# Softmax times V on one core: two heads side by side on the partitions, in two score buffers of 64 KB

## The chip, the cores and the metric

The kernel runs on one core of a Trainium2 chip. A core has a matrix engine (TensorE: PE in the profile, PEld for its weight loads), a vector engine (VectorE, DVE), an activation engine (ScalarE, ACT), a general engine (GpSimd, POOL), and a queue (SyncE, SP) that here issues every DMA; 16 DMA engines carry the transfers. SBUF and PSUM are addressed by 128 partitions. The metric is the device time of one execution in microseconds, the median of several runs.

## The reference

```python
batch, n_heads, seq, head_dim = 8, 12, 1024, 64      # scores: (8, 12, 1024, 1024), v: (8, 12, 1024, 64), float32
def reference(scores, v):
    scores_max = np.max(scores, axis=-1, keepdims=True)
    attn = np.exp(scores - scores_max)
    attn = attn / (np.sum(attn, axis=-1, keepdims=True) + 1e-8)
    return np.matmul(attn, v).astype(np.float32)
```

There are 96 heads. Each has 4 MB of scores, 256 KB of v and 256 KB of output.

## The kernel before

The kernel exponentiates the scores without subtracting the maximum, in fp16, and divides by the row sums after the product with v; a column of ones beside v gives the sums. It notes the extremes of the sums and of v, and if a later test (`judge`, then `count`) says that they left the range in which this is safe, a slow general path (`general`) runs instead. With these inputs it does not.

A loop over 24 iterations handles four heads each (`AHEAD = 4`, k = 0 to 3). Each head has a score buffer `s_nat[k]` of 128 partitions by 8 rows of 1024 (32 KB a partition; partition p holds 8 adjacent rows of the head). For each head, with r from 0 to 7 (one "row" is 128 score rows, one on each partition):

- ScalarE exponentiates two rows at a time from `s_nat` into one of 8 buffers `p_nat` (L414); for the last head of an iteration, from its third row on, one row at a time.
- TensorE turns the eight 128x128 blocks of a row into a PSUM bank `psT` (L427, four buffers). The identity used, `order16`, also puts even partitions first and odd ones behind.
- VectorE copies the bank to `pt` in SBUF (L434, four buffers).
- Three rows later (`LAG = 3`), `finish` multiplies: eight products of 128x65 into `psO` (L173), which collects four rows in a bank (`G = 4`).
- After four rows, VectorE takes reciprocals of the sums (L150) and scales (L158): two instructions of 64 partitions x 256 each, into `out_sb`, which holds two heads.

POOL spreads v from the form in which it was loaded (`v_sb`, four heads in 1 MB) to `vones[k]`, an fp16 copy with ones (`spread_v`, L270: four copies a head). `watch_v` (L287) reduces each `vones[k]` to its largest magnitude on VectorE, for the test.

SP's queue issues in an order written out by hand (`queue`): load of head 0 and of head 1 for the next iteration, the store of the heads 0 and 1, load of head 2, v, load of head 3, the store of the heads 2 and 3. A load into `s_nat[k]` waits until ScalarE has read the whole buffer, and each load is one DMA of 4 MB. Only in the last iteration but one are the heads 2 and 3 of the last iteration loaded in parts: 4, 4, then 3, 2, 1, 1 and 1 rows (`last`). In the last iteration, `end` scales the last head by ScalarE (L216) and VectorE (L219) and stores its output in two DMAs (L227).

TensorE's instructions are kept in program order (`in_line`). At the end of an iteration `judge` computes a count on VectorE and TensorE, and ScalarE loads its table again when the next begins (ACT_TABLE_LOAD).

Of the kernel before, what the change touches and what calls it, by code (L numbers as in the profile page):

```python
# [26 lines left out]
def kernel(  # L27
# [14 lines left out]
    R = SQ // P  # L42
    C = SK // P
    M = D + 1
    EB = 2
    G = 4
# [5 lines left out]
    T = 2  # L52

    sc_bh = scores.rearrange("b h (p r) j -> (b h) p r j", p=P)
    v_bh = v.rearrange("b h (i t) d -> (b h i) (t d)", i=Q)  # L60


    W = P // T
    out_bh = out.rearrange("b h (j x) d -> (b h j) (x d)", j=W)

# [6 lines left out]
    order16 = const_pool.tile([P, P], FP16, name="order16")  # L72

    nc.vector.tensor_copy(
        out=order16[:].rearrange("p (t j) -> p t j", t=T),
        in_=ident32[:].rearrange("p (j t) -> p t j", t=T),
    )


    vones_bufs = []  # L80
    for k in range(AHEAD):
        vo = const_pool.tile([P, C, D + 2], FP16, name=f"vones{k}")
        nc.vector.memset(vo[:, :, D : D + 2], 1.0)
        vones_bufs.append(vo)


# [10 lines left out]
    seen = small_pool.tile([P, 1 + AHEAD * R + 1], FP32, name="seen")  # L97
    nc.vector.memset(seen, 1.0)
    done = small_pool.tile([P, R * D], FP32, name="done")
    v_seen = small_pool.tile([P, 1 + AHEAD + 1], FP32, name="v_seen")  # L100
    nc.vector.memset(v_seen, 1.0)
    psT_bufs = buffers(ps_pool, 4, [P, SK], FP16, "psT")


    psO_bufs = buffers(ps_pool, 2 * (R // G), [P, 512], FP32, "psO")
# [32 lines left out]
    def one(bh, n):  # L138
        return bh[bass.ds(n, 1)].rearrange("o p r d -> (o p) r d")

    def sums(k, st, b):

        psO = st["psO"][b][:, 0 : G * M].rearrange("p (g m) -> p g m", m=M)
        at = 1 + k * R + b * G
        recip = seen[:, at : at + G].rearrange("p (g o) -> p g o", o=1)
        return psO, recip

    def invert(k, st, b):
        psO, recip = sums(k, st, b)
        return nc.vector.reciprocal(out=recip, in_=psO[:, :, D : D + 1])  # L150

    def normalise(k, st, b):

        psO, recip = sums(k, st, b)
        h = k % T
        for t in range(T):
            part = slice(t * W, (t + 1) * W)
            nc.vector.tensor_tensor(  # L158
                out=st["out_sb"][h * W : (h + 1) * W, t, b * G : (b + 1) * G, :],
                in0=psO[part, :, 0:D],  # L160
                in1=recip[part].to_broadcast([W, G, D]),
                op=mybir.AluOpType.mult,
            )

    def finish(u):

        n0, k, r, pt, st = u
        b, g = r // G, r % G
        if r == 0:
            st["out_sb"] = out_bufs[k // T]  # L170
        bank = st["psO"][b]
        for c in range(C):
            product = nc.tensor.matmul(  # L173
                out=bank[:, g * M : (g + 1) * M],
                lhsT=pt[:, c * P : (c + 1) * P],
                rhs=st["vones"][:, c, 0:M],
                start=(c == 0),
                stop=(c == C - 1),
            )
            in_line(product)  # L180
        if g == G - 1 and k < AHEAD - 1:
            invert(k, st, b)
            normalise(k, st, b)
        if r == R - 1:
            spread_v(k)
            if k == T - 1:
                store(n0, 0)

    def store(n0, k):

        to = out_bh.rearrange("(m x) y -> m x y", x=P)[bass.ds((n0 + k) // T, 1)]
        to = to.rearrange("o x y -> (o x) y")
        of = out_bufs[k // T][:].rearrange("x t r d -> x (t r d)")
        send(nc.sync.dma_start(out=to, in_=of))
# [9 lines left out]
    def end(st):  # L204


        k, h = AHEAD - 1, (AHEAD - 1) % T
        send(
            nc.sync.dma_start(
                out=out_bh[(BH - T) * W : (BH - T + h) * W],  # L210
                in_=out_bufs[k // T][0 : h * W].rearrange("x t r d -> x (t r d)"),
            )
        )
        psO, recip = sums(k, st, 0)
        for g in range(G):
            nc.scalar.mul(done[:, g * D : (g + 1) * D], psO[:, g, 0:D], recip[:, g, :])  # L216
        invert(k, st, 1)
        psO, recip = sums(k, st, 1)
        nc.vector.tensor_tensor(  # L219
            out=done[:, G * D :].rearrange("p (g d) -> p g d", d=D),  # L220
            in0=psO[:, :, 0:D],
            in1=recip.to_broadcast([P, G, D]),
            op=ALU.mult,
        )
        to = out_bh[(BH - 1) * W : BH * W].rearrange("j (t y) -> t j y", t=T)
        for t in range(T):
            send(nc.sync.dma_start(out=to[t], in_=done[t * W : (t + 1) * W]))  # L227

    stores = []
    writers = {}  # L230
# [14 lines left out]

    def load(k, n, parts=(R,), r=0, **cond):
        for rows in parts:
            queue(
                nc.sync.dma_start(  # L249
                    out=s_bufs[k][:, r : r + rows, :],  # L250
                    in_=one(sc_bh, n)[:, r : r + rows, :],
                    **cond,
# [14 lines left out]
    def spread_v(k):  # L267

        for s in range(S):
            spread = nc.gpsimd.tensor_copy(  # L270
                out=vones_bufs[k][s * Q : (s + 1) * Q, :, 0:D].rearrange(
                    "i (h l) d -> i h l d", l=L
                ),
                in_=v_sb[k * Q : (k + 1) * Q, :, s],
            )
            for watch in watches:
                apart(spread, watch, "products in between")

    def spread_of(tile, n):

        nc.vector.tensor_reduce(out=tile[:, 0:1], in_=tile[:, 0 : n + 1], axis=X, op=ALU.min)  # L281
        nc.vector.tensor_reduce(  # L282
            out=tile[:, n + 1 : n + 2], in_=tile[:, 1 : n + 2], axis=X, op=ALU.max
        )

    def watch_v(k, behind):
        watch = nc.vector.tensor_reduce(  # L287
            out=v_seen[:, 1 + k : 2 + k],
            in_=vones_bufs[k][:, :, 0:D],
            axis=mybir.AxisListType.XY,  # L290
# [5 lines left out]

    def within(out, tile, n, low, high, also=None):
        part = small("part")
        if also is None:
            nc.vector.tensor_scalar(  # L300
                out=part, in0=tile[:, n + 1 : n + 2], scalar1=high, scalar2=None, op0=ALU.is_le
            )
        else:
            nc.vector.scalar_tensor_tensor(  # L304
                out=part, in0=tile[:, n + 1 : n + 2], scalar=high, in1=also,
                op0=ALU.is_le, op1=ALU.mult,
            )
        nc.vector.scalar_tensor_tensor(  # L308
            out=out, in0=tile[:, 0:1], scalar=low, in1=part, op0=ALU.is_ge, op1=ALU.mult
        )  # L310
# [190 lines left out]
```

## Time and profile before

| | |
|---|---|
| median of 3 runs | 1067.54 us (1067.52 to 1068.3) |
| profiled execution | 1067.78 us; its span 1066.0 us |
| granted TensorE clock, mean | 0.825 |
| HBM read, written | 436.21 MB, 25.17 MB; 433 GB/s over the span |
| DMA queue q1 | 99.1% of 16 engines' span |
| busiest engine, VectorE | 786.2 us (74%) |
| ScalarE | 741.1 us (70%) |

The span runs from the first to the last instruction of the profiled execution; the execution's time also holds what lies around it. In the page's second part each digit is the busy share of one of 40 slices of the span, in tenths. In its fourth part the chain is followed backwards from the last instruction. A group's row gives the line, the engine, the operation, what it writes and reads, the count, then the busy time, the mean duration in ns, and the idle time of the engine just before with what ended it. In a time line the first two numbers are the start and the length in us, and brackets give the idle time before it and what ended it.

### The profile page before, as it was taken

How to read it: one execution, taken by the hardware profiler on the slowest of the kernel's cores; microseconds unless marked ns; L12 is line 12 of the kernel's file. 1: busy time of each engine (PE TensorE's matmuls, PEld its weight loads, DVE VectorE, ACT ScalarE, POOL GpSimd, SP SyncE). 2: the span in 40 equal slices, each digit the busy share in tenths (PEclk: the TensorE clock that was granted, in tenths of full speed). 3: DMA queues.
4: the chain of work that ended last, by engine and by line, in shares of the span. 5: the costliest groups of instructions: out<-in, count | busy, mean ns of one | idle time of the engine just before them, and what ended most of it. 6: DMA issues, size and time to landing. Idle time of an engine off the chain costs nothing.

```text
span 1066.0 us, 33658 instructions
## 1 busy us (share of the span) xinstructions
PE 727.3 (68%) x12312; PEld 692.9 (65%) x12312; DVE 786.2 (74%) x1660; ACT 741.1 (70%) x484; POOL 244.8 (23%) x406
## 2 busy tenths in 40 slices
PE   2766866677766667676676766767766667666775
PEld 2766756666766667666675766667765667666674
DVE  1876867868678677776777777868677677786786
ACT  3756776666867668586676776666767668586685
POOL 3113212131121311212113211131121311212113
PEclk9888888878788888887888888878788787887888
DMA  9999999999999999999999999999999999999995
GB/s 393 431 423 434 424 438 430 432 432 428 432 433 433 429 436 433 433 433 432 434 427 439 433 433 433 431 435 432 433 432 433 422 440 433 432 432 427 434 427 206
DMA packets 25014, 453.08 MB, mean 425 GB/s; under 512 B 2800, under 2 KB 2800, under 8 KB 9392
## 3 DMA queue, kind: packets, MB, share of 16 engines
q1 hardware_dynamic: 25008, 453.00, 99.1%
q8 instruction: 4, 0.07, 0.0%
q14 instruction: 2, 0.02, 0.0%
HBM read 436.21 MB, written 25.17 MB: 433 GB/s over the span
## 4 chain that ended last, share of the span: by engine, by line
DMA 61%; PE 11%; PEld 8%; ACT 5%; DVE 5%; issue 4%; POOL 2%; SPq 1%; POOLq 1%; ACTq 0%; DVEq 0%
DMA s_nat<-in_scores_dram 61%; PE psT L427 6%; ACT p_nat L414 5%; PE psO L173 5%; PEld L427 5%; DVE pt L434 5%; PEld L173 4%; POOL vones L270 2%; SPq L261 1%; SPq L249 0%; POOLq L270 0%; POOLq L385 0%; POOLq L461 0%; POOLq L389 0%; DVE out_sb L158 0%
## 5 line engine op out<-in xcount | busy, mean ns | idle before, releaser
L414 ACT ACTIVATE p_nat<-s_nat 128x2048 f16<-128x2048 f32 (+1 forms) x456 | 709.4, 1630 | 219.0 <-DMA s_nat<-in_scores_dram 173.2
L427 PE MATMUL psT<-order,p_nat 128*128 128x128 f16 x6144 | 570.3, 251 | 227.5 <-ACT p_nat L414 216.3
L434 DVE COPY pt<-psT 128x1024 f16<-128x1024 f16 x768 | 513.9, 687 | 189.1 <-PE L173 77.3
L427 PEld LDWEIGHTS <-p_nat 128*128 128x128 f16 x6144 | 461.3, 125 | 244.8 <-ACT p_nat L414 232.6
L270 POOL CAST vones<-v_sb 32x512 f16<-32x512 f32 x400 | 244.1, 610 | 814.1 <-PE L427 385.0
L173 PE MATMUL psO<-vones,pt 128*128 128x65 f16 x6144 | 358.5, 205 | 34.6 <-DVE pt L434 33.0
L173 PEld LDWEIGHTS <-pt 128*128 128x128 f16 x6144 | 301.2, 106 | 48.7 <-DVE pt L434 42.6
L158 DVE TENSOR_TENSOR out_sb<-psO,seen 64x256 f32<-64x256 f32 x380 | 160.2, 422 | 63.6 <-DMA out_dram<-out_sb 52.4
L414 ACT ACT_TABLE_LOAD x24 | 30.8, 1283 | 94.1 <-PE psO L173 52.8
L287 DVE TENSOR_REDUCE v_seen<-vones 128x1 f32<-128x512 f16 x96 | 65.1, 679 | 0.8
L324 PE MATMUL psO<-vones,right 128*1 128x1 f16 x24 | 3.9, 164 | 69.2 <-DVE right L308 69.2
L324 PEld LDWEIGHTS <-right 128*1 128x1 f16 x24 | 1.9, 79 | 72.2 <-DVE right L308 72.2
L150 DVE RECIPROCAL seen<-psO 128x4 f32<-128x4 f32 x192 | 33.7, 176 | 8.6 <-PE psO L173 8.6
L308 DVE SCALAR_TENSOR_TENSOR right<-seen,part 128x1 f16<-128x1 f32 x24 | 10.5, 437 | 0.8
L308 DVE SCALAR_TENSOR_TENSOR fits<-v_seen,part 128x1 f32<-128x1 f32 x24 | 10.0, 415 | 0.0
L328 DVE CAST count<-psO 1x1 int32<-1x1 f32 x24 | 3.5, 146 | 6.2 <-PE psO L324 6.2
L304 DVE SCALAR_TENSOR_TENSOR part<-seen,fits 128x1 f32<-128x1 f32 x24 | 4.6, 192 | 0.8
L281 DVE TENSOR_REDUCE seen<-seen 128x1 f32<-128x33 f32 x24 | 4.5, 187 | 0.8
L281 DVE TENSOR_REDUCE v_seen<-v_seen 128x1 f32<-128x5 f32 x24 | 3.8, 159 | 0.7
L282 DVE TENSOR_REDUCE seen<-seen 128x1 f32<-128x33 f32 x24 | 4.2, 177 | 0.0
L282 DVE TENSOR_REDUCE v_seen<-v_seen 128x1 f32<-128x5 f32 x24 | 3.6, 149 | 0.0
L300 DVE TENSOR_SCALAR part<-v_seen 128x1 f32<-128x1 f32 x24 | 3.5, 144 | 0.0
(12 smaller groups left out, 2.8 us busy)
## 6 DMA issues: line engine op xcount, KB each, us to landing
s_nat<-in_scores_dram SPq DMA_DIRECT2D x96, 4096.0 KB, 32.3
v_sb<-in_v_dram SPq DMA_DIRECT2D x24, 1024.0 KB, 18.5
out_dram<-out_sb SPq DMA_DIRECT2D x47, 512.0 KB, 26.2
s_nat<-in_scores_dram SPq DMA_DIRECT2D x2, 2048.0 KB, 31.3
s_nat<-in_scores_dram SPq DMA_DIRECT2D x1, 1536.0 KB, 32.2
s_nat<-in_scores_dram SPq DMA_DIRECT2D x3, 512.0 KB, 20.7
s_nat<-in_scores_dram SPq DMA_DIRECT2D x1, 1024.0 KB, 25.1
out_dram<-out_sb SPq DMA_DIRECT2D x1, 256.0 KB, 3.0
```

The lines of the kernel that those rows point to most:

```text
L150: return nc.vector.reciprocal(out=recip, in_=psO[:, :, D : D + 1])
L158: nc.vector.tensor_tensor(out=st["out_sb"][h * W : (h + 1) * W, t, b * G : (b + 1) * G, :], in0=psO[part, :, 0:D], in1=recip[part].to_broa ...
L173: product = nc.tensor.matmul(out=bank[:, g * M : (g + 1) * M], lhsT=pt[:, c * P : (c + 1) * P], rhs=st["vones"][:, c, 0:M], start=(c == 0) ...
L261: nc.sync.dma_start(out=v_sb[:].rearrange("x h s l d -> x (h s l d)"), in_=rows[bass.ds(n // AHEAD, 1)].rearrange("o x y -> (o x) y"),)
L270: spread = nc.gpsimd.tensor_copy(out=vones_bufs[k][s * Q : (s + 1) * Q, :, 0:D].rearrange("i (h l) d -> i h l d", l=L), in_=v_sb[k * Q : ( ...
L281: nc.vector.tensor_reduce(out=tile[:, 0:1], in_=tile[:, 0 : n + 1], axis=X, op=ALU.min)
L282: nc.vector.tensor_reduce(out=tile[:, n + 1 : n + 2], in_=tile[:, 1 : n + 2], axis=X, op=ALU.max)
L287: watch = nc.vector.tensor_reduce(out=v_seen[:, 1 + k : 2 + k], in_=vones_bufs[k][:, :, 0:D], axis=mybir.AxisListType.XY, op=ALU.max, appl ...
L308: nc.vector.scalar_tensor_tensor(out=out, in0=tile[:, 0:1], scalar=low, in1=part, op0=ALU.is_ge, op1=ALU.mult)
L414: exp = nc.scalar.activation(out=p_nat[:, g : g + rows, :].rearrange("p r (x v) -> p x r v", v=Q * L), in_=s_bufs[k][:, r + g : r + g + ro ...
L427: turned = nc.tensor.transpose(out=psT[:, c * P : (c + 1) * P], in_=p_row[:, c // L, c % L, :], identity=order16[:],)
L434: copy = nc.vector.tensor_copy(out=pt[:], in_=psT[:])
```

## The change

Two heads now lie beside each other: partitions 0 to 63 hold one head and 64 to 127 the next, with 16 adjacent score rows on each partition. So there are two buffers of 128 x 16 x 1024 (64 KB a partition, 8 MB) instead of four of 32 KB, and an iteration of four heads has two passes, k = 0 and 1 (`K = 2`), of R = 16 rows.

- A load is one DMA of 8 MB. The first, before the loop, comes in halves; the last, for k = 1 of the last iteration, in 4, 4, 3, 2, 1, 1, 1 rows. SP's order is now: load of k = 0, its store, load of k = 1, its store, v.
- `vones` is one tile with the values of both heads of a pass side by side, each with its ones. A product is 128x130: every score row is multiplied by both heads' values, and only the half that belongs to its head is read afterwards.
- Three rows of 130 columns fill a bank of `psO` (`G = 3`), so a pass has six groups, the last of one row. Each group has a reciprocal and two scalings, 64 partitions x 192 (or x 64).
- `psT` and `pt` become two buffers of two rows each (two banks of PSUM), and VectorE copies two rows in one instruction, but for the last eight rows of k = 1, which are exponentiated and copied one at a time.
- `order16` gives way to a plain identity. `watch_v` becomes one reduction over all of `vones` in each iteration with two small tests behind it. The last pass is scaled by the ordinary `normalise`, and stored in two DMAs: 12 rows, then 4.

```diff
-    R = SQ // P
-    G = 4
+    G = 3
+    K = AHEAD // T
+    W = P // T
+    R = SQ // W
+    N = D + 2
+    M = T * N - 2
+    GROUPS = -(-R // G)
...
-    s_bufs = buffers(sb_pool, AHEAD, [P, R, SK], FP32, "s_nat")
+    s_bufs = buffers(sb_pool, K, [P, R, SK], FP32, "s_nat")
...
-    pt_bufs = buffers(sb_pool, 4, [P, SK], FP16, "pt")
-    out_bufs = buffers(sb_pool, 2, [P, T, R, D], FP32, "out_sb")
+    pt_bufs = buffers(sb_pool, 2, [P, EB, SK], FP16, "pt")
+    out_bufs = buffers(sb_pool, K, [P, R, D], FP32, "out_sb")
...
-    psT_bufs = buffers(ps_pool, 4, [P, SK], FP16, "psT")
+    psT_bufs = buffers(ps_pool, 2, [P, EB, SK], FP16, "psT")
...
-                rhs=st["vones"][:, c, 0:M],
+                rhs=vones[:, k, c].rearrange("p t n -> p (t n)")[:, 0:M],
...
-        if g == G - 1 and k < AHEAD - 1:
-            invert(k, st, b)
-            normalise(k, st, b)
-        if r == R - 1:
+        if i == G - 1 or r == R - 1:
+            normalise(k, st, g)
+        if r == R - 1 and k < K - 1:
             spread_v(k)
-            if k == T - 1:
-                store(n0, 0)
+            store(n0, k)
...
             with tc.If(n0 < BH - 2 * AHEAD) as cmp2:
                 queued[:] = before
-                load(AHEAD - 2, (n0 + (2 * AHEAD - 2)) % BH)
-                load_v((n0 + 2 * AHEAD) % BH)
-                load(AHEAD - 1, (n0 + (2 * AHEAD - 1)) % BH)
-                store(n0, AHEAD - T)
+                load(k, (n0 + (AHEAD + T * k)) % BH)
+                store(n0, k)
+                load_v((n0 + 2 * AHEAD) % BH)
             with cmp2.Else():
                 queued[:] = before
-                load(AHEAD - 2, BH - 2, (4, 4))
-                load(AHEAD - 1, BH - 1, (3,))
-                store(n0, AHEAD - T)
-                load(AHEAD - 1, BH - 1, (2, 1, 1, 1), 3)
+                load(k, BH - T, (4, 4, 3))
+                store(n0, k)
+                load(k, BH - T, (2, 1, 1, 1), 11)
...
+                late = k == K - 1 and r >= R // 2
                 if r % EB == 0:
-                    p_nat = take(p_bufs)
-                    rows = 1 if k == AHEAD - 1 and r > 0 else EB
+                    p_nat, psT2, pt2 = take(p_bufs), take(psT_bufs), take(pt_bufs)
+                    rows = 1 if late else EB
...
-                copy = nc.vector.tensor_copy(out=pt[:], in_=psT[:])
-                rewrite(pt, copy)
...
+                if late:
+                    copy = nc.vector.tensor_copy(out=pt, in_=psT)
+                    rewrite(pt2, copy)
+                    other_bank(psT2, r % EB, copy)
+                elif r % EB == EB - 1:
+                    copy = nc.vector.tensor_copy(out=pt2[:], in_=psT2[:])
+                    rewrite(pt2, copy)
+                if k == 0 and r == R // 2 - 1:
+                    watch_v(copy)
+                if r == R - 1 and k < K - 1:
+                    load(k, (n0 + (AHEAD + T * k)) % BH, cond=n0 < BH - AHEAD)
```

More of the change, by code (lines that the diff above doesn't have):

```diff
@@ L158, in normalise @@
             nc.vector.tensor_tensor(
[L159 to L162, printed above, removed]
+                out=out_bufs[k][part, g * G : g * G + rows, :],
+                in0=psO[part, :, t * N : t * N + D],
+                in1=recip[part].to_broadcast([W, rows, D]),
+                op=ALU.mult,
             )
@@ L295, in watch_v @@
         watches.append(watch)
[L297 to L301, printed above, removed]
-            )
[L303 to L310, printed above, removed]
+        for bound, op in ((V_MIN, ALU.is_ge), (V_MAX, ALU.is_le)):
+            nc.vector.scalar_tensor_tensor(
+                out=fits, in0=most, scalar=bound, in1=fits, op0=op, op1=ALU.mult
+            )
     def small(name, dtype=FP32):
@@ L449, in heads @@
             finish(pending.pop(0))
-        last(n0, st)
-        spread_of(seen, AHEAD * R)
+        last(n0)
         judge(st["psO"][-1])
-    assert BH % AHEAD == 0 and BH >= 2 * AHEAD and SK == Q * S * C
+    assert BH % AHEAD == 0 and BH >= 2 * AHEAD and SK == Q * S * C and K == 2
     load_v(0)
-    for k in range(AHEAD):
-        load(k, k)
-    for k in range(AHEAD):
+    for k in range(K):
+        load(k, T * k, (R // 2, R // 2) if k == 0 else (R,))
+    for k in range(K):
         spread_v(k)
@@ L466 @@
         heads(n0)
-    good = nc.values_load(count[:], min_val=0, max_val=P)
+    good = nc.values_load(
+        count[:], min_val=0, max_val=P,
+        skip_runtime_bounds_check_because="a count of partitions, which is compared and no address",
+    )
     with tc.If(good < P, preferred_fallthrough_block=False):
```

207 lines of the change are left out of this document (87 added, 120 removed).

## The prediction

> **What bounds the kernel now.** I read the page first, for the busy shares and the DMA row.
>
> ```profile
> PE 727.3 (68%) x12312; PEld 692.9 (65%) x12312; DVE 786.2 (74%) x1660; ACT 741.1 (70%) x484; POOL 244.8 (23%) x406
> DMA  9999999999999999999999999999999999999995
> DMA packets 25014, 453.08 MB, mean 425 GB/s; under 512 B 2800, under 2 KB 2800, under 8 KB 9392
> DMA 61%; PE 11%; PEld 8%; ACT 5%; DVE 5%; issue 4%; POOL 2%; SPq 1%; POOLq 1%; ACTq 0%; DVEq 0%
> s_nat<-in_scores_dram SPq DMA_DIRECT2D x96, 4096.0 KB, 32.3
> ```
>
> No engine is full; the DMA is, in 39 of 40 slices. A 4 MB load takes 32.3 us from issue to landing, although it moves in about 9.7 us: over 20 us of other transfers are queued ahead of it. Then the chain in order of time, near its end, which gives the period.
>
> ```profile
> 938.44 27.30 DMA s_nat<-in_scores_dram
> 965.85 1.92 ACT p_nat L414
> ...
> 982.31 27.11 DMA s_nat<-in_scores_dram
> 1009.53 1.92 ACT p_nat L414
> ```
>
> The fourth load of an iteration lands at 965.74 and, one iteration on, at 1009.42: 43.68 us. An iteration moves four loads of 4.194 MB, two stores of 0.524 MB and one v load of 1.049 MB, 18.87 MB, so 432 GB/s. At that rate a load is 9.71 us, a store 1.21, v 2.43. What a transfer costs is thus its bytes, and the end of the program is the end of this stream plus what the engines still have to do when the last data come. The time line of ScalarE shows that part.
>
> ```profile
> 1009.53 7.60 ACT L414 ACTIVATE p_nat<-s_nat 128x2048 f16<-128x2048 f32 x7 [4.85 <-DMA s_nat<-in_scores_dram]
> 1020.40 1.28 ACT L414 ACT_TABLE_LOAD   x1 [3.27 <-PE psO L173]
> 1021.69 7.32 ACT L414 ACTIVATE p_nat<-s_nat 128x2048 f16<-128x2048 f32 x4
> 1030.09 17.50 ACT L414 ACTIVATE p_nat<-s_nat 128x2048 f16<-128x2048 f32 x10 [1.08 <-PE psT L427]
> 1048.45 4.85 ACT L414 ACTIVATE p_nat<-s_nat 128x1024 f16<-128x1024 f32 x5 [0.87 <-PE L173]
> ```
>
> The last iteration starts its exponentials at 1021.69, when its first head has landed (1009.42 + a store + a load = 1020.3) and the table is loaded. From there ScalarE hardly rests, and no wait names a DMA: the last iteration is a compute run, and its start decides the end. Its last normalisation and store:
>
> ```profile
> 1057.10 0.42 DVE L219 TENSOR_TENSOR done<-psO,seen 128x256 f32<-128x256 f32 x1
> 1057.60 1.12 SPq L227 DMA_DIRECT2D out_dram<-done  x2
> ```
>
> So first exponential to last product scaled is 1057.52 - 1021.69 = 35.83 us, and 8.5 us more to the span's end at 1066.0. That execution took 1067.78 us, 1.78 more than its span; the median is 0.24 lower.
>
> **Loads in pieces of 8 MB.** Per iteration the same bytes move, in two score loads instead of four. In mid-run the question is whether the queue stays fed. Pair A lands at t; its eight exponentials of two rows are 8 x 1.9 = 15.2 us (7.32 us for four in a row makes it 14.6), so A's buffer is free and its next load issued at about t + 15.7. The queue meanwhile brings B (19.42, behind a store), then a store and v (3.64), and needs A's next load at t + 24.3. The lead is 8.5 us, against more than 20 before. For B, whose second half is eight one-row exponentials (0.965 us each: 139.0/144), 4 x 1.83 + 8 x 0.965 = 15.0, and the lead is about 8. The store of k = 0 stands ahead of B's load on SP, but waits only for products that finish some 6 us after B landed; the v load waits for POOL's 8 copies of 0.61 us behind the last product, and the queue gets to it 20 us later. I cost all this at nothing; what hides it is the 8 us of queued transfers, and each us beyond them would cost up to two us an iteration.
>
> At the end the grain shows. In the stream v(23) now comes behind B of iteration 22, so that B lands at 1009.42 - 2.43 = 1006.99. Behind it come a store, v and the whole 8 MB of A for the last iteration: 1006.99 + 1.21 + 2.43 + 19.42 = **1030.05**. Before, ScalarE had worked since 1021.69 on the first head alone. Now no row of the last 32 can begin before 1030.05: **+8.4 us** on the path. The last B comes in parts, and lands by about 1052 as now, ahead of its use.
>
> **VectorE per iteration.** Rows from the groups by form:
>
> ```profile
> L434 DVE COPY pt<-psT 128x1024 f16<-128x1024 f16 x768 | 513.9, 687 | 189.1 <-PE L173 77.3 <-PE L427 63.3 <-PE psO L173 38.5
> L158 DVE TENSOR_TENSOR out_sb<-psO,seen 64x256 f32<-64x256 f32 x380 | 160.2, 422 | 63.6 <-DMA out_dram<-out_sb 52.4 <-SPq L389 0.7
> L287 DVE TENSOR_REDUCE v_seen<-vones 128x1 f32<-128x512 f16 x96 | 65.1, 679 | 0.8
> L150 DVE RECIPROCAL seen<-psO 128x4 f32<-128x4 f32 x192 | 33.7, 176 | 8.6 <-PE psO L173 8.6
> ```
>
> Reciprocal (4 elements, 176 ns) and scaling (256, 422 ns) give about 1 ns an element and 0.16-0.17 us fixed. A copy of 2048: 1.22 us if the fixed part is paid once, 1.37 if it is two copies; I take 1.22, since the fixed part shows in every row. Copies: 32 x 0.687 = 22.0 becomes 12 x 1.22 + 8 x 0.687 = 20.1 (21.9 at 1.37). Scaling: 16 x 0.422 = 6.8 becomes 20 of 192 at 0.355 and 4 of 64 at 0.222, 8.0. Reciprocals: 8 become 12, +0.7. The watch: 4 x 0.679 = 2.7 becomes one of 2048 elements, 512 at 0.679 scaled, 2.28. The two small tests on fits replace six small ones, -0.1 to -0.4. Sum -1.9 + 1.2 + 0.7 - 0.4 - 0.2 = -0.6, and up to +1.2 with the dear copies; before, copies standing one behind another also overlapped (513.9/768 = 0.669), which fewer, longer ones do less, up to +0.8. I take +0.5, and -0.6 to +2 as bounds. It lies beside the DMA in 23 iterations and on the path in the last.
>
> **TensorE.** 6144 products go from 65 to 130 columns. A transposition of 128 columns is the nearest row: warm, eight take 0.45 us in the chain, against 0.25 for eight products. A row of both goes from 0.70 to 0.90 us, 32 rows to 29 us an iteration; and about double (0.85 for eight transpositions in the chain at 1012.97) for some 4 us behind each wait for data. Under 43.7 us it is hidden. On the path it only adds in the filling of the pipe: a copy now waits for two rows of transpositions, cold 0.85 us more before the first copy; two pairs of buffers instead of four singles let a copy start only when two rows' products are done, which I put at 1 us over the iteration (0 to 2).
>
> **ScalarE** runs 20 exponentials an iteration instead of 19, +0.1 us. The table load stays and lies before the landing.
>
> **Sum.** Last iteration, first exponential to last scaling: 35.83 + 0.5 + 0.85 + 1.0 + 0.1 = 38.3, from 1030.08: 1068.4, where it was 1057.5: +10.8. One last 128 KB store (2.3 us to landing) replaces two issued in turn: -0.6. The four products of ScalarE in end() go, off the path. The start keeps its 4 MB first landing and its wait for POOL's 16 copies: 0. Together +10.2: span 1076.2, execution 1078.0, median about **1077.8**. The other edits (the identity in plain order, the memsets before the loop, the general path, which does not run) touch nothing that the chain names: 0.
>
> Packets double from 32 to 64 KB if they are not split. By the trace's packet records a 4 KB packet lasts 159 ns and a 32 KB one 1213, which leaves 8.4 ns fixed; 8 fewer per engine for each pair, 48 pairs, 3.2 us at most. Loads land 9.68 us apart, which is 1210 ns a packet, so part of it already overlaps. I take 0 and keep -3.2.
>
> The page "SBUF — State Buffer" of the Trainium skill (section on the DMA setup-cost knee) puts about 2 us on every transfer and tells to coalesce: 48 transfers fewer would be 96 us off. The trace does not agree: queued loads of 4 MB land 9.68 us apart, 433 GB/s, with no room for 2 us; it stays as a part of rival 3.
>
> **The rivals.** (1) *VectorE's chain becomes the bound.* Compute alone needs about 38.3 us and 1.3 of table load an iteration, 40 to 41 with the waits between. The first exponential of all is at 18.06; with a compute period P the last iteration starts at 18.06 + 23 P, so it decides from P = (1030.05 - 18.06)/23 = 44.0 on, and each 0.1 us of P is 2.3 us. P of 44.2 to 45.2 gives 1082 to 1105. For: 3 to 4 us of margin, and a cold TensorE at both landings. Against: the work adds only 0.5. 10%.
>
> (2) *The queue runs dry.* If ScalarE is held by 10 us (p_nat released late), 1 to 2 us at 24 reloads: 1102 to 1126. Against: 16 rows of p_nat. 4%.
>
> (3) *The stream itself shortens*, in the s_nat loads, by fewer boundaries between transfers. It must exceed 12.4 us, 0.26 per pair, to end faster than before by our bound; the packet fit gives 3.2. At 0.3 a pair, 14.4: 1063.4. 5%.
>
> (4) *The late grain costs nothing*, since the run was held by something else in the last iteration: then +1 or +2, 1068 to 1069. Against: ScalarE's unbroken row above. 3%.
>
> (5) *The rate falls with the wider address step*: 64 KB between neighbouring partitions. The slowest rate in the trace is that of 4 KB packets, 25.8 GB/s an engine against 27.0 at 32 KB: 4.6% of 931 us of score loads would be 43 us more, 1121. That longer packets only got faster speaks against it. 3%. The Trainium skill's "DMA: Bandwidth & Descriptors" (its table row on HBM row pitch) has 207 against 214 GB/s at a pitch of 512 KiB; no run here shows such a loss.
>
> **How the numbers follow.** Forecast 75%, its own range 1070 to 1086 from the bounds (-3.2 packets, -1.1 VectorE, -1 buffers; upwards the dear copies, buffers, cold rows, 6 to 8). The likeliest is 1077.8. Downwards the range takes in (4) from 1068; upwards the lower half of (1), to 1092; outside lie about 2 in 10. About 0.2%, 2.1 us, is what a measurement can tell from no change: faster 0.05 from (3), same 0.04 from (4) and the edge of the forecast, slower 0.91.
>
> **What would show it.** Right: the DMA row full to the last two slices, iteration period 43.7 us, two landings of 19.4 us each; the last iteration's first exponential at 1030, by a DMA wait; last scaling at 1067 to 1070; copies of 128x2048 at 1.22 us. Wrong: a DMA row with gaps, or periods over 44 (1 or 2); a first exponential of the last iteration well before 1028 (3); a last compute run shorter than 36 us or longer than 42.

## The result: 1074.31 us, and the profile after

The changed kernel takes 1074.31 us (median of 6 runs, 1073.7 to 1074.57); the kernel before, beside it, 1068.38 us (6 runs, 1067.52 to 1069.47). The ratio is 1.0054, 95% interval 1.0044 to 1.0065: slower by 5.9 us, where +10.2 was predicted. The profiled execution took 1074.52 us, its span 1072.8 us (before 1066.0). The spans lie 6.8 us apart, the medians 5.9, since the profiled execution of the kernel before (1067.78) was one of its shorter ones.

The page, its busy shares, the DMA row, the packets, the chain by engine and the loads:

```profile
PE 793.8 (74%) x12312; PEld 757.8 (71%) x12312; DVE 768.7 (72%) x1539; ACT 737.2 (69%) x504; POOL 239.2 (22%) x399
DMA  9999999999999999999999999999999999999991
DMA packets 18436, 453.06 MB, mean 422 GB/s; under 512 B 2048, under 2 KB 2176, under 8 KB 8704
DMA 60%; ACT 27%; issue 7%; PE 2%; DVE 1%; PEld 1%; ACTq 1%; SPq 0%; DVEq 0%
s_nat<-in_scores_dram SPq DMA_DIRECT2D x47, 28.4
```

The DMA is full in the same 39 slices, with the same bytes in 6578 fewer packets. What changed is the chain: ScalarE's share went from 5% to 27%. TensorE is busier by 66.5 us and VectorE less busy by 17.5, and neither bounds the kernel over the whole span. The chain in order of time shows the period and what follows each landing:

```profile
956.97 27.47 DMA s_nat<-in_scores_dram
984.81 1.01 issue
986.30 1.34 issue
987.64 12.72 ACT p_nat L368 x7
1000.58 27.52 DMA s_nat<-in_scores_dram
1028.47 1.01 issue
1029.96 1.34 issue
1031.29 1.91 ACT p_nat L368
```

The first pair of an iteration lands at 984.44 and, one iteration on, at 1028.10 (start and length added). Over many iterations the period is 43.59 us on the mean, against 43.68 before. ScalarE's time line shows what now stands behind each of these landings:

```profile
984.53 1.28 ACT L368 ACT_TABLE_LOAD   x1 [8.10 <-DMA s_nat<-in_scores_dram]
985.83 14.53 ACT L368 ACTIVATE p_nat<-s_nat 128x2048 f16<-128x2048 f32 x8
1005.11 14.91 ACT L368 ACTIVATE p_nat<-s_nat 128x2048 f16<-128x2048 f32 x12 [4.76 <-PE psT L381]
1028.18 1.28 ACT L368 ACT_TABLE_LOAD   x1 [8.17 <-DMA s_nat<-in_scores_dram]
1029.48 29.32 ACT L368 ACTIVATE p_nat<-s_nat 128x2048 f16<-128x2048 f32 x20
```

ScalarE sat idle for 8.17 us ahead of the last iteration and began its exponentials at 1029.48; before, it began at 1021.69. The table load waits for the landing too, so its 1.28 us stand on the path. From there the 20 exponentials run on. VectorE's time line gives the other end of that run:

```profile
1026.39 0.15 DVE L292 CAST count<-psO 1x1 int32<-1x1 f32 x1 [0.26 <-PE psO L288]
1033.38 1.23 DVE L393 COPY pt<-psT 128x2048 f16<-128x2048 f16 x1 [6.84 <-PE L381]
1041.33 2.29 DVE L250 TENSOR_REDUCE most<-vones 128x1 f32<-128x2048 f16 x1
1067.53 0.47 DVE L140 TENSOR_TENSOR out_sb<-psO,seen 64x64 f32<-64x64 f32 x2
```

The count (the last work of iteration 22) is done at 1026.5, so VectorE was 6.8 us idle, too; the first copy starts at 1033.38 and the last scaling ends at 1068.0. The last iteration's first copy before the change:

```profile
1025.45 0.69 DVE L434 COPY pt<-psT 128x1024 f16<-128x1024 f16 x1 [1.30 <-PE L427]
```

The groups by form give the new sizes:

```profile
L393 DVE COPY pt<-psT 128x2048 f16<-128x2048 f16 x288 | 352.4, 1224 | 266.7 <-PE L381 170.0
L140 DVE TENSOR_TENSOR out_sb<-psO,seen 64x192 f32<-64x192 f32 x480 | 170.4, 355 | 14.9
L250 DVE TENSOR_REDUCE most<-vones 128x1 f32<-128x2048 f16 x24 | 54.9, 2286 | 0.8
L152 PE MATMUL psO<-vones,pt 128*128 128x130 f16 x6144 | 486.2, 223 | 63.0 <-DVE fits L260 40.4
```

So the 6.8 us of the span split in three (us):

| stretch | before | after | measured | predicted |
|---|---|---|---|---|
| start to the first exponential of the last iteration | 1021.69 | 1029.48 | +7.8 | +8.4 |
| from there to the end of the last scaling | 35.83 | 38.53 | +2.7 | +2.45 |
| from there to the end of the span | 8.5 | 4.8 | -3.7 | -0.6 |

The first two are near what was foretold; the third is not. It has two parts. The last store landed 3.0 us behind the last scaling before the change (at 1060.49) and 1.9 behind it after (at 1069.91), which is -1.1. The other -2.6 lie between VectorE's branch over the general path and the end of the span: 3.8 us before (from 1062.15), 1.2 after (from 1071.59). VectorE's records show its drain (its next instruction) behind that branch: before at 1065.19, 3.04 us later; after at 1071.81, 0.22 later. That pause is 2.8 us shorter, but not all of it reaches the end, since SyncE's drain now comes behind VectorE's, at 1072.07. The DMA view of the end of each kernel (from 1060 us on; queue and kind: packets, MB, share of the engines) shows what went with it. First before, then after:

```profile
q14 instruction: 2, 0.02, 0.4%
q8 instruction: 1, 0.02, 0.4%
q1 hardware_dynamic: 15, 0.00, 0.1%
```

```profile
q1 hardware_dynamic: 288, 0.52, 8.4%
q8 instruction: 1, 0.02, 0.4%
```

Two packets of 8 KB of instructions on queue q14 (by the records one at 1063.17, in VectorE's pause, and one at 1065.77, 0.6 us behind it) are not there in the changed kernel.

### The profile page after: what moved, and what is told of

The parts are those of the page before. It is cut to its first block, busy times and chain, and to the rows that moved or that the text cites. A ratio compares the mean times of both kernels' runs of the same rounds, so it can differ in the third digit from the quotient of the medians.

```text
span 1072.8 us, 32527 instructions
## 1 busy us (share of the span) xinstructions
PE 793.8 (74%) x12312; PEld 757.8 (71%) x12312; DVE 768.7 (72%) x1539; ACT 737.2 (69%) x504; POOL 239.2 (22%) x399
## 2 busy tenths in 40 slices
DMA packets 18436, 453.06 MB, mean 422 GB/s; under 512 B 2048, under 2 KB 2176, under 8 KB 8704
## 4 chain that ended last, share of the span: by engine, by line
DMA 60%; ACT 27%; issue 7%; PE 2%; DVE 1%; PEld 1%; ACTq 1%; SPq 0%; DVEq 0%
DMA s_nat<-in_scores_dram 60%; ACT p_nat L368 27%; PE psT L381 1%; PE psO L152 1%; ACTq L368 1%; DVE pt L393 1%; PEld L381 0%; PEld L152 0%; DVE most L250 0%; ACT L368 0%; SPq L219 0%; DVE pt L389 0%; DVE out_sb L140 0%; DVE seen L132 0%; DVE seen L276 0%
## 5 line engine op out<-in xcount | busy, mean ns | idle before, releaser
L381 PE MATMUL psT<-ident,p_nat 128*128 128x128 f16 x6144 | 506.0, 233 | 171.0 <-ACT p_nat L368 171.0
L381 PEld LDWEIGHTS <-p_nat 128*128 128x128 f16 x6144 | 425.6, 119 | 181.0 <-ACT p_nat L368 181.0
L393 DVE COPY pt<-psT 128x2048 f16<-128x2048 f16 x288 | 352.4, 1224 | 266.7 <-PE L381 170.0
L152 PE MATMUL psO<-vones,pt 128*128 128x130 f16 x6144 | 486.2, 223 | 63.0 <-DVE fits L260 40.4
L152 PEld LDWEIGHTS <-pt 128*128 128x128 f16 x6144 | 387.3, 99 | 84.8 <-DVE pt L393 55.8
L140 DVE TENSOR_TENSOR out_sb<-psO,seen 64x192 f32<-64x192 f32 (+1 forms) x576 | 191.8, 333 | 18.0
L389 DVE COPY pt<-psT 128x1024 f16<-128x1024 f16 x192 | 123.5, 685 | 2.3
L250 DVE TENSOR_REDUCE most<-vones 128x1 f32<-128x2048 f16 x24 | 54.9, 2286 | 0.8
L132 DVE RECIPROCAL seen<-psO 128x3 f32<-128x3 f32 (+1 forms) x288 | 49.3, 171 | 2.8 <-PE L381 0.8
L260 DVE SCALAR_TENSOR_TENSOR fits<-most,fits 128x1 f32<-128x1 f32 x48 | 7.4, 155 | 0.0
```

The costliest lines, as they stand in the source:

```text
L140: nc.vector.tensor_tensor(out=out_bufs[k][part, g * G : g * G + rows, :], in0=psO[part, :, t * N : t * N + D], in1=recip[part].to_broadcas ...
L152: product = nc.tensor.matmul(out=st["psO"][g][:, i * M : (i + 1) * M], lhsT=pt[:, c * P : (c + 1) * P], rhs=vones[:, k, c].rearrange("p t ...
L250: watch = nc.vector.tensor_reduce(out=most, in_=vones[:, :, :, :, 0:D].rearrange("p k c t d -> p k (c t) d"), axis=mybir.AxisListType.XYZ, ...
L260: nc.vector.scalar_tensor_tensor(out=fits, in0=most, scalar=bound, in1=fits, op0=op, op1=ALU.mult)
L381: turned = nc.tensor.transpose(out=psT[:, c * P : (c + 1) * P], in_=p_row[:, c // L, c % L, :], identity=ident16[:],)
L389: copy = nc.vector.tensor_copy(out=pt, in_=psT)
```

## The experiments

Each kernel was timed in five rounds beside the kernel before, so ratios are to that; differences to the changed kernel use its 1074.31 us. The median of the kernel before lay between 1068.38 and 1068.99 us in the four groups of runs, so such a difference is uncertain by about 0.6 us.

The theory was that the grain of the last loads (how much has to land before work can start) costs about 8 us, that the longer compute run of the last iteration costs 2 to 3, and that the end gains back 3 by something in the way out of the program. Rivals were that the wide products or a slower stream cost part of it.

**1. The first pair's load in halves.** Each load of k = 0 becomes two DMAs of 4 MB.

```diff
-                    load(k, (n0 + (AHEAD + T * k)) % BH, cond=n0 < BH - AHEAD)
+                    load(k, (n0 + (AHEAD + T * k)) % BH, (R // 2, R // 2), cond=n0 < BH - AHEAD)
```

> The changed kernel, but the load of k = 0 comes in two halves of 8 rows in every iteration, as the very first one does. Theory (the grain of the load sets when the last iteration starts): the first half of the last iteration lands some 9.7 us ahead of the second, near 1019; then not the landing but the end of the iteration before (its products at about 1025.5, then the table load) holds the first exponential, which moves from 1029.5 to about 1027; the end comes 2 to 3.5 us earlier, 1071 to 1072. Packets of half of the loads are 32 KB again, which gives back up to 1 us. Rival (the end is set by the end of the DMA stream or by VectorE's total, whenever the run starts): 1074 to 1075.

Measured: 1072.19 us, ratio 1.0034 [1.0022, 1.0046], 2.1 us less than the changed kernel. ScalarE, and then VectorE:

```profile
1006.02 14.91 ACT L368 ACTIVATE p_nat<-s_nat 128x2048 f16<-128x2048 f32 x12 [12.88 <-DMA s_nat<-in_scores_dram]
1020.94 1.28 ACT L368 ACT_TABLE_LOAD   x1
1022.24 24.59 ACT L368 ACTIVATE p_nat<-s_nat 128x2048 f16<-128x2048 f32 x15
```

```profile
1029.05 0.15 DVE L292 CAST count<-psO 1x1 int32<-1x1 f32 x1 [0.26 <-PE psO L288]
1031.36 1.23 DVE L393 COPY pt<-psT 128x2048 f16<-128x2048 f16 x1 [2.16 <-PE L381]
```

The time came as expected, by another way. The exponentials start 7.2 us earlier, at 1022.24, and no longer wait for data. But the second pair of iteration 22 still comes in one piece, and ScalarE starts on it 0.9 us later (1006.02 instead of 1005.11). That iteration now ends later, at 1029.2 on VectorE instead of 1026.5 (the other 1.8 us were not taken apart), and the first copy of the last one gains only 2.0 us. The wait moved from ScalarE to the engines behind it.

**2. The old general path in the changed kernel.** The change also rewrote the general path, which does not run: a fill moved from VectorE to GpSimd, copies and a scaling from VectorE to ScalarE, and its loop got the register-based synchronisation. Here all of that is put back, to find VectorE's shorter pause.

```diff
-        nc.gpsimd.memset(s_bufs[0][:, 3, 0 : C * (D + 1)], 1.0)
+        nc.vector.memset(s_bufs[0][:, 3, 0 : C * (D + 1)], 1.0)
...
-                nc.scalar.copy(out=pt[:, h * half : (h + 1) * half], in_=psO_bufs[h][:, 0:half])
+                nc.vector.tensor_copy(out=pt[:, h * half : (h + 1) * half], in_=psO_bufs[h][:, 0:half])
...
```

> The changed kernel with the general path, which does not run, written as before (its work on VectorE instead of ScalarE and GpSimd, its loop without the register-based synchronisation). Theory (VectorE's jump over the longer general path is what cost 3 us between its branch at 1062.15 and its drain at 1065.19 in the kernel before): 2.5 to 3 us slower, 1077. Rival (the shorter end comes from the left-out bounds check, or from the last stores): 1074.3, no change.

Measured: 1074.61 us, 1.0054 [1.004, 1.0067]. Nothing changed, no pause came back.

**3. The old bounds check of the count.**

```diff
-    good = nc.values_load(
-        count[:], min_val=0, max_val=P,
-        skip_runtime_bounds_check_because="a count of partitions, which is compared and no address",
-    )
+    good = nc.values_load(count[:], min_val=0, max_val=P)
```

> The changed kernel with the bounds check on the loaded count as before. Theory (the jump over the general path): no change, 1074.3, at most +0.5 for the check itself. Rival (the check made the end long): 2.5 to 3 us slower, 1077.

Measured: 1074.75 us, 1.0059 [1.0045, 1.0072]. No pause came back either. The theory that one of these two edits makes VectorE's pause fell.

**4. Products of 65 columns.** This kernel leaves out the products with the other head's values, and so does not compute the reference's output.

```diff
-                rhs=vones[:, k, c].rearrange("p t n -> p (t n)")[:, 0:M],
+                rhs=vones[:, k, c, c % 2, 0 : D + 1],
```

> The changed kernel with products of 65 columns instead of 130: it leaves out the products with the other head's values (the values it takes alternate between the heads, so its output is not the reference's). Theory (VectorE, not TensorE, sets the pace of the last iteration, and in the others the DMA): 0 to 1 us faster, 1073.3 to 1074.3. Rival (the wider products lie on the path of the last iteration, 32 rows of 0.2 us): 4 to 6 us faster, 1068 to 1070.

Measured: 1074.26 us, 1.0052 [1.0039, 1.0066]. The page's busy shares:

```profile
PE 680.1 (63%) x12312; PEld 627.3 (58%) x12312; DVE 768.1 (72%) x1539; ACT 737.3 (69%) x504; POOL 239.2 (22%) x399
```

TensorE is 114 us less busy and the time is the same. Taking both heads' values in each product costs nothing here. The chain of the changed kernel names TensorE from 1051.25 to 1065.72 of the last iteration; by this run that is not where its length comes from, and VectorE's time line has no gap of more than 0.2 us there.

**5. The kernel before with the new general path and without the bounds check.**

```diff
-        nc.vector.memset(s_bufs[0][:, 3, 0 : C * M], 1.0)
+        nc.gpsimd.memset(s_bufs[0][:, 3, 0 : C * M], 1.0)
...
-                nc.vector.tensor_copy(out=pt[:, h * half : (h + 1) * half], in_=psO_bufs[h][:, 0:half])
+                nc.scalar.copy(out=pt[:, h * half : (h + 1) * half], in_=psO_bufs[h][:, 0:half])
...
-    good = nc.values_load(count[:], min_val=0, max_val=P)
+    good = nc.values_load(
+        count[:], min_val=0, max_val=P,
+        skip_runtime_bounds_check_because="a count of partitions, which is compared and no address",
+    )
```

> The kernel before with the general path and the count's load written as in the changed kernel (no bounds check; nothing else changed). Theory (VectorE's 3.0 us between its branch at 1062.15 and its drain at 1065.19 come from these lines, both together): about 2.8 us faster, 1066. Rival (the pause belongs to the layout of the whole program before, for instance the branches of end() and last()): 0 to 0.5 us faster, 1068.4.

Measured: 1068.03 us, 0.9998 [0.9989, 1.0007]. VectorE still pauses, from 1062.35 to 1065.51, with the two packets on q14 (at 1063.64 in the pause and at 1066.09 behind it). Together with 2 and 3: neither edit makes the pause or takes it away.

**6. The grain alone, in the kernel before.** The loads of heads 0 and 1 are issued together, head 1's first, so that the last iteration's first head lands behind both.

```diff
-        if k < AHEAD - 2:
-            load(k, (n0 + (AHEAD + k)) % BH, cond=n0 < BH - AHEAD)
+        if k == 1:
+            for j in (1, 0):
+                load(j, (n0 + (AHEAD + j)) % BH, cond=n0 < BH - AHEAD)
```

> The kernel before with the loads of heads 0 and 1 in the other order in the queue, so that head 0, which every iteration begins with, lands only when both have landed, as with one load of 8 MB. Nothing else changes: products of 65 columns, single copies, packets of 32 KB. Theory (the grain of the first load sets when the last iteration starts): its first exponential moves from 1021.7 to the second landing, 1030.0, or 1031.3 if the table load waits for it too; the run of 35.8 us stays: 8 to 9.7 us slower, 1077 to 1078. Rival (the last iteration's length makes up for a late start, since ScalarE then has both heads at once): 0 to 4 us slower.

Measured: 1077.25 us against 1068.65 in the same job, 1.0083 [1.007, 1.0097]: +8.6 us from the order of two DMAs in each iteration, with the engines' work and every size and packet as before, and the same period (43.68). ScalarE, and VectorE's last scaling:

```profile
1030.62 1.28 ACT L415 ACT_TABLE_LOAD   x1 [12.93 <-DMA s_nat<-in_scores_dram]
1031.91 29.25 ACT L415 ACTIVATE p_nat<-s_nat 128x2048 f16<-128x2048 f32 x19
```

```profile
1066.62 0.42 DVE L219 TENSOR_TENSOR done<-psO,seen 128x256 f32<-128x256 f32 x1
```

It is the picture of the changed kernel: idle until all 8 MB are there, table load behind the landing, then one unbroken run (35.1 us to the end of the last scaling, at 1067.04). The first exponential is 10.2 us later than in the kernel before and the run 0.7 us shorter. This shows that the late first row of the last iteration costs 8 us by itself.

**7. The watch ahead of the first copy.** The reduction over all values (2.29 us) and its two tests move to before the iteration's first copy, where VectorE is idle, from behind the fourth.

```diff
+                    if k == 0 and r == EB - 1:
+                        watch = watch_v()
                     copy = nc.vector.tensor_copy(out=pt2[:], in_=psT2[:])
+                    if k == 0 and r == EB - 1:
+                        after(copy, watch)
                     rewrite(pt2, copy)
-                if k == 0 and r == R // 2 - 1:
-                    watch_v(copy)
```

> The changed kernel with the watch over vones (2.29 us) and its two small tests placed before the first copy of an iteration, where VectorE sits idle, and not behind the fourth copy. Theory (VectorE's work sets the length of the last run): the last scaling comes 2 to 2.5 us earlier, 1072. Rival (ScalarE's exponentials or the products set it): 1073.8 to 1074.3.

Measured: 1072.31 us, 1.0039 [1.0025, 1.0052], 2.0 us less than the changed kernel. VectorE:

```profile
1026.61 0.15 DVE L292 CAST count<-psO 1x1 int32<-1x1 f32 x1 [0.26 <-PE psO L288]
1030.27 2.29 DVE L250 TENSOR_REDUCE most<-vones 128x1 f32<-128x2048 f16 x1 [3.52 <-POOL vones L239]
1033.58 1.22 DVE L395 COPY pt<-psT 128x2048 f16<-128x2048 f16 x1 [0.63 <-PE L381]
```

The watch ends before the first copy could start, and the last scaling ends at 1065.29 instead of 1068.01. From the first exponential (1029.68) that is 35.6 us, no more than before the change. In the last iteration VectorE's work, one instruction behind another, sets the length; with experiment 4, TensorE's does not.

**8. Both old edits at the end together** (2 and 3 in one kernel).

```diff
-                nc.scalar.copy(out=pt[:, h * half : (h + 1) * half], in_=psO_bufs[h][:, 0:half])
+                nc.vector.tensor_copy(out=pt[:, h * half : (h + 1) * half], in_=psO_bufs[h][:, 0:half])
...
-        skip_runtime_bounds_check_because="a count of partitions, which is compared and no address",
```

> The changed kernel with both the general path and the bounds check as before. Theory (both together cause VectorE's pause): 2.5 to 3.5 us slower than 1074.3, 1077 to 1078. Rival (layout of the whole program): at most 0.7 slower, 1075.

Measured: 1075.28 us, 1.0062 [1.0049, 1.0076]; no pause, 1.0 us from the changed kernel, with intervals that overlap. From VectorE's branch to the end of the span it takes 1.7 us where the changed kernel takes 1.2: SyncE, with its check, ends last.

**9. All loads in halves.** As 1, and the loads of k = 1 too, the first one before the loop included.

```diff
-                load(k, (n0 + (AHEAD + T * k)) % BH)
+                load(k, (n0 + (AHEAD + T * k)) % BH, (R // 2, R // 2))
```

> The changed kernel with all loads of 8 MB, of k = 0 and of k = 1, in two halves of 8 rows. Theory (the grain costs twice: the last iteration but one ends late since its k = 1 lands whole, and the last begins late since its k = 0 lands whole): the last iteration's transpositions begin near 1020 instead of 1031, VectorE then needs its 35 to 37 us, last scaling at 1058 to 1061 instead of 1068; with the short end 1065 to 1068, after 2 us more of DMA stream by 32 KB packets. That would be faster than the kernel before. Rival (only the first landing matters, or VectorE's backlog is always there): as with one half, 1071 to 1072.

Measured: 1068.84 us, 1.0003 [0.9994, 1.0012]: 5.5 us less than the changed kernel, level with before, not ahead of it, so the expectation was missed. ScalarE, then VectorE:

```profile
997.50 3.72 ACT L368 ACTIVATE p_nat<-s_nat 128x2048 f16<-128x2048 f32 x2 [3.61 <-PE psT L381]
1007.16 11.31 ACT L368 ACTIVATE p_nat<-s_nat 128x2048 f16<-128x2048 f32 x10 [5.93 <-DMA s_nat<-in_scores_dram]
1020.54 1.28 ACT L368 ACT_TABLE_LOAD   x1 [2.08 <-PE L381]
1021.84 7.32 ACT L368 ACTIVATE p_nat<-s_nat 128x2048 f16<-128x2048 f32 x4
```

```profile
1026.09 0.14 DVE L292 CAST count<-psO 1x1 int32<-1x1 f32 x1 [0.26 <-PE psO L288]
1028.45 1.23 DVE L393 COPY pt<-psT 128x2048 f16<-128x2048 f16 x1 [2.21 <-PE L381]
1062.78 0.47 DVE L140 TENSOR_TENSOR out_sb<-psO,seen 64x64 f32<-64x64 f32 x2
```

The exponentials start at 1021.84, as before the change (1021.69), and the first copy is 4.9 us earlier than in the changed kernel. Two things keep it from more. The packets are 32 KB again and the period is 43.67. And ScalarE stands 5.93 us at the fifth row of iteration 22's second pair (1001.2 to 1007.2), although the first half had landed: in the branch for the last loads the parts are 4, 4 and 3 rows, so one wait that serves all cases must name the second half for row 4.

**10. Forty dead VectorE instructions in the general path of the changed kernel.**

```diff
             nc.vector.reciprocal(out=den, in_=den)
+            for _ in range(40):
+                nc.vector.tensor_scalar(
+                    out=den, in0=den, scalar1=1.0, scalar2=None, op0=ALU.mult
+                )
```

> The changed kernel with 40 more VectorE instructions in the general path, which does not run. Theory (the 3 us pause of the kernel before is a load of instructions: two packets of 8 KB of the kind instruction at 1063.17 and 1065.77, which the changed kernel lacks since VectorE's program is shorter, 128 against 158 instructions): VectorE's jump over the longer path needs such a load, 2.5 to 3.5 us slower, 1077 to 1078, with such packets near the end. Rival (length and distance do not matter): 1074.3 to 1074.7, no packets.

Measured: 1076.41 us, 1.0072 [1.0058, 1.0086], 2.1 us more than the changed kernel (the intervals of the two ratios overlap a little, but the fastest run here, 1076.0, lies above the slowest there, 1074.57). VectorE's records have the pause again, branch at 1071.48 and drain at 1074.33, 2.85 us; its last scaling ends at 1067.89, as without the edit, and the span at 1075.0 instead of 1072.8. The DMA view of its end:

```profile
q8 instruction: 1, 0.02, 0.5%
q14 instruction: 2, 0.02, 0.3%
```

The two packets on q14 are back (one near 1072.5, in the pause, and one near 1074.9, behind it). Only VectorE's program grew, so what went away was a load of its instructions at the jump over the general path; that the packets are VectorE's is read from this and from their times. Built from the kernels of these runs and with every kind of instruction counted (128 and 158 in the expectation are another, smaller count), VectorE's program has 181 instructions in the changed kernel, and 184 and 185 in kernels 2 and 8, all without the pause; it has 220 in the kernel before, 216 in kernel 5 and 261 here, all with it.

**11. Halves, with the last loads cut to match.** As 9, and the last pair's parts are 8 and 3 rows instead of 4, 4 and 3, so that row 4 can wait for the first half.

```diff
-                load(k, BH - T, (4, 4, 3))
+                load(k, BH - T, (R // 2, 3))
```

> As with both loads in halves, but the last load of k = 1 begins with 8 and 3 rows instead of 4, 4 and 3, so that the wait of its fifth row no longer names the second half in every iteration (with both halves ScalarE stood 5.93 us at its fifth row for a DMA). Theory (grain): the last iteration but one ends at 1020 to 1022 instead of 1026, the last scaling near 1058 to 1060 instead of 1063.3; 1064.5 to 1066, faster than the kernel before by 0.25% to 0.4%. Rival (VectorE's backlog, not the landing, ends the last iteration but one): no better than 1068.8.

Measured: 1069.56 us, 1.0006 [0.9997, 1.0015]; the expectation was missed. ScalarE:

```profile
1022.10 1.28 ACT L368 ACT_TABLE_LOAD   x1 [4.83 <-DMA s_nat<-in_scores_dram]
1031.79 7.32 ACT L368 ACTIVATE p_nat<-s_nat 128x2048 f16<-128x2048 f32 x4 [1.07 <-PE psO L152]
1042.86 14.92 ACT L368 ACTIVATE p_nat<-s_nat 128x2048 f16<-128x2048 f32 x12 [3.75 <-PE psT L381]
```

The mended wait did what it was to do: iteration 22 ended at 1022.5 on VectorE, 3.7 us earlier than in kernel 9. But the data came later: the first half of the last k = 0 pair landed at 1022.0, since the period had gone from 43.67 to 43.84 from about the twelfth iteration on, and in the last iteration ScalarE stood 3.75 us until the part of 8 rows had landed (1042.76; the row names TensorE, but the wait of the same length in kernel 12 is put down to the DMA). The last scaling ended at 1063.11, near that of kernel 9 (1063.25).

The landing records say where the period comes from. Each transfer leaves sixteen of them, and it has landed with the last. Up to about the eleventh iteration all sixteen come every 43.67 us. From the twelfth on fifteen still do, and the last falls behind by 0.16 us an iteration: of the first half of the last k = 0 pair, fifteen parts were there by 1020.24 and the sixteenth at 1022.01 (in kernel 9, 1020.32 and 1020.46). So it is not the whole stream that slows but one sixteenth of it, for which every landing waits.

**12. As 11, with the watch behind the second copy.**

```diff
-                if k == 0 and r == R // 2 - 1:
+                if k == 0 and r == 2 * EB - 1:
                     watch_v(copy)
```

> The run before this one in the list, with the watch moved behind the second copy of an iteration, where VectorE waits 1 to 2 us for TensorE. Theory (VectorE sets the length of the last run): 1 to 2 us faster than that run, 1063 to 1065, the fastest of all. Rival: no change to it.

Measured: 1071.96 us (1070.63 to 1073.39; the profile is of the slowest), 1.0028 [1.0018, 1.0038]; missed again, and by the same two steps, larger: a period of 43.94 from the twelfth iteration on, the first half at 1023.3, the part of 8 rows at 1044.07. Again fifteen records of a landing keep 43.67 (fifteen parts of that first half were there by 1020.21), and the last falls behind, here by 0.25 us an iteration. Why one part lags in 11 and 12 is open. Up to iteration 22 they issue the very transfers of kernel 9, so it is not the cut of the transfers: only the engines' waits, with them the moments at which loads are issued, and in 12 the place of the watch differ until then. No version here beat the kernel before; 5, 9 and 11 are level with it.

## Why the prediction was right, and where it was not

- **The grain, +8.4 predicted.** Right in mechanism and nearly in size (+7.8): experiment 6 has it alone, +8.6 us, and 9, with its loads in halves, takes 5.5 us back. Two errors inside the term nearly cancel. "I take 0 and keep -3.2" for the longer packets: the trace's packet records show that 64 KB packets do occur, 5888 of them at 2418 ns (the median) against 2 x 1213 for two of 32 KB, and the period fell by 0.09 us, 2.0 us over 23 iterations; the bound held it, the value did not. And "The table load stays and lies before the landing" is wrong: it waits for the same data and stands behind the landing, 1.28 us and 0.1 of issue on the path.
- **The last run, +2.45 predicted.** +2.7 measured; that the sum is so near is luck. The 0.85 us for a later first copy measured 0.14 (from the first exponential to the first copy 3.76 us before, 3.90 after), and the way from there to the last scaling grew by 2.6 us where the other terms have 1.6. VectorE's work fell by 0.7 us an iteration (busy 786.2 and 768.7 us in 24), as the sum of its rows said (-0.6) and not as was taken (+0.5). The single rows are right: the copy of 2048 (1.22 us predicted, 1.224 measured), the scaling (0.355 for 192) and the watch (2.28 and 2.286); paying the fixed part once was the right choice. What the sum did not say is that VectorE sets this stretch. It took the watch as 0.4 us less work; experiment 7 shows that its place in the order is worth 2.0 us, nearly its whole length, and with it moved the way from the first copy to the last scaling is 31.7 us, no longer than before the change (32.1).
- **TensorE, hidden.** Right: 114 us less of its work in experiment 4 leave the time as it is.
- **The queue stays fed, cost nothing.** Right: the DMA row is as full as before, and ScalarE's waits of 8 us stand between iterations, not in the queue.
- **The end, -0.6 predicted, -3.7 measured.** This is the step that failed, and it makes nearly all of the 3.5 us between 1077.8 and 1074.3. The one last store gave 1.1, not 0.6. The other 2.6 sit under "The other edits (... the general path, which does not run) touch nothing that the chain names: 0." Code that does not run is still jumped over. Experiment 10 puts the pause back by adding instructions that are never executed, and its two packets of instructions with it; 2, 3, 5 and 8 show that it is not this or that edit in the general path, and with the counts given there they point to how long VectorE's whole program is: the path jumped over is the old one in 2 and 8, without the pause, and the new one in 5, with it. The Trainium skill has the mechanism in "Runtime: NRT & Kernel Launch" (section on instruction fetch mechanics): a taken branch to a target outside the two blocks that an engine holds must fetch it before going on. The traces agree in that the jump goes on only after a packet of instructions has come in, and the price is theirs: a pause of 2.85 to 3.2 us, of which 2.1 show in the time of experiment 10. Some 0.5 of the 2.6 came back with SyncE's bounds check and the old path in 8.
- **The rivals.** (1) and (2) did not happen: no gap in the DMA row, a period under 43.7. (3) is there in kind, at 2.0 us where 12.4 were needed. (4) and (5) are out by experiment 6 and by the period. The lower end of the range, 1070, is more than its own bounds add up to (1077.8 - 3.2 - 1.1 - 1 = 1072.5); the measured 1074.3 lies inside either way.

Left open: the exact place from which the jump needs a load (between 185 and 216 instructions of VectorE here), and why one sixteenth of the stream lags in experiments 11 and 12.

## What to carry to other kernels

In a kernel bound by its stream of data, a larger transfer saves little in mid-run and is paid at the end: no work of the last iteration can start before its whole first transfer has landed, so count the time from there, and consider cutting the transfers there (cutting those of the last iteration alone was not tried). When a transfer is cut, follow the wait to every row and every case of the program: in experiments 1 and 9 it moved to the next engine or the next part. Where a landing drifts, look at its parts: it waits for the slowest of sixteen. Add up the way from the last useful instruction to the end as carefully as the rest, code that is only jumped over included.

## What the runs showed of the hardware that was not expected

- A jump over a general path that does not run costs VectorE 0.22 us or about 3 us, by the length of its program; in the dear case one 8 KB packet of instructions on q14 lies in the pause and one behind it. In the time of the kernel that is 2.1 us (experiment 10), against 5.9 for the whole change.
- Packets of 64 KB exist and are a little cheaper than two of 32 KB: 2418 ns against 2426 (medians). Two loads fewer in an iteration gave 0.09 us, so a queued load of 4 MB carries next to no fixed cost.
- ScalarE's table load at the head of an iteration takes part in the first wait for data; where the data are late, its 1.28 us come on top (1028.18 here, 1030.62 in experiment 6).
- With the same transfers and a queue that is always full, one part in sixteen of every transfer can begin to lag in mid-run, by 0.16 us an iteration in experiment 11 and 0.25 in 12, while the other fifteen keep their period of 43.67. The landings follow the slowest part: every 43.84 and 43.94 us. The cause was not found.
